# Rotation tables of the state-space batches in two buffers, outputs of a batch behind the next one's chunk inputs, four tiles for the gates

## The chip, the cores and the metric

One NeuronCore of a Trainium2 chip runs the whole kernel. The metric is device time in microseconds (us), the median of a few runs. TensorE is called PE here (its weight loads PEld), VectorE DVE, ScalarE ACT, GpSimd POOL, and the queue that issues most transfers SP. Each engine works through its own list of instructions in order, and engines wait for each other at semaphores.

## The reference, cut to what matters

One encoder layer over 16 meta tokens and 1024 tokens, in float32: a norm, one wide projection `w_in`, a state-space mixer (S5), differential attention, a gated sum of the two, and a feed-forward block. The change lies in the mixer and in the gate columns of the projection.

```
proj = hn @ w_in[layer]                      # columns: u 512, q, k 1024 each, v 1024, gates 2 x 1024
g_s5 = sigmoid(proj[..., OFF_GS:OFF_GA]);  g_attn = sigmoid(proj[..., OFF_GA:IN_COLS])
y = s5_mixer(u, ...)                         # 32 groups of 16 channels, 64 complex states, 2 directions
  bu_re, bu_im = einsum('blgc,gpc->lbgp', ug, b_re[dr]), einsum(..., b_im[dr])
  xr, xi = coef * bu                         # complex
  s = associative_scan(a * s_prev + x)       # along the 1040 tokens; reversed for direction 1
  y_dir = einsum(sr, c_re) - einsum(si, c_im)
y = gelu(y + d_skip * u)
```

## The kernel before, in words

The mixer is blocked: 1040 tokens are 130 chunks (`NJ`) of 8, and the 32 groups are worked through in **8 batches** of 4 groups. A batch is a generator, `s5_batch`, cut by `yield` into nine steps, called s0 to s8 here:

- **s0**: PE multiplies `Gm` (input matrix) and `c1` into `pk`; ACT copies it to `kt`. **s1**: PE transposes `Gm` (`pg`), ACT copies to `GT`; POOL builds the next batch's `Gm` (6 instructions, lines 541 to 543).
- **s2**: POOL builds `Hm` (6 instructions); SP moves `kt` into `M` (8 transfers); PE computes the chunk inputs `px`, ACT copies them to `Xr`, `Xi` (8 copies); SP loads the next batch's `U` (8 transfers).
- **s3**: DVE rotates `Xr`, `Xi` by the tables `TC`, `TS` (cosine and sine of each chunk's phase): six instructions of 128x520, called *the rotation*; then 8 scans. **s4**: DVE rotates back and writes `Sx`, 16 instructions of some 256 elements (*the Sx work*).
- **s5**: POOL builds the next batch's `TC` and `TS` by doubling (`s5_table`): 2 memsets and 48 instructions, most of them tiny. **s6**: PE transposes `M`, ACT copies it to `MT`.
- **s7**: PE sums `py` from `MT`, `Hm` and `Sx`; ACT squares, DVE multiplies. **s8**: ACT's Tanh, DVE writes `yt`, SP stores it to `yd` (4 transfers).

`TC` and `TS` have one buffer each, as have `Gm`, `Hm`, `M`, `Xr`, `Xi`; `U` and `yt` have two. Batch 0's table is built on DVE, the others on POOL.

The order is written out by hand. The steps of all batches make one list, `side`; from batch 1 on, s0 and s1 of a batch stand ahead of s7 and s8 of the batch before. `weave` hands one side step out after about each half-step of the main list, which is PE's own work: gate units 0 to 5 (`gate_steps`, 8 half-steps of 12 matmuls each), two value units (`v_steps`, *the V steps* here), gate unit 6. So every step has a place on every engine's list. A gate group ends in ACT's Tanh into `gt` (two buffers, pool `vg`); units 0 to 3 add DVE's +1.

Each unit's weights are split ahead of time into `wh` (ACT cast) and `wl` (a 128x1024 subtraction, line 174, on DVE): `unit` places the two halves of the next unit's split inside the present one. The unit ahead of the first gate unit is `U_U[1]`, woven with `s5_params` (the `gen_p` steps), a long run of small DVE instructions that ends in `dd`. The pool `utp` holds `ut`, the staging tile of the state-space inputs on their way to `ud` in memory.

Of the kernel before, what the change touches and what calls it, by code (L numbers as in the profile page):

```python
# [9 lines left out]
F32 = mybir.dt.float32  # L10
# [17 lines left out]
NJ = L // 8  # L28
# [23 lines left out]
def tile_hybrid_encoder(ctx, tc, A, out, dbg=None, stop=None):  # L52
    nc = tc.nc
# [74 lines left out]
    def weave(main, *sides, part=1.0):  # L128

        total = part * sum(w for w, _ in main)  # L130
        done = [0] * len(sides)
        t = 0.0
        for w, fn in main:
            fn()
            t += w
            for i, s in enumerate(sides):
                while done[i] < len(s) and done[i] + 1 <= len(s) * t / total + 1e-9:
                    s[done[i]]()
                    done[i] += 1
        for i, s in enumerate(sides):  # L140
            for fn in s[done[i]:]:
                fn()

    def steps_of(gen, n):

        return [lambda: next(gen, None) for _ in range(n)]
# [17 lines left out]
    def w_hi_part(i, h):  # L164
        if i < len(wviews):
            if h == 0:
                wtile[i] = (wp.tile([128, 2, 1024], F32R, tag="wh", name=f"wh{i}"),
                            wp.tile([128, 2, 1024], F32R, tag="wl", name=f"wl{i}"))
            nc.scalar.copy(wtile[i][0][:, h], wtile[i, h])

    def w_lo_part(i, h, eng):
        if i < len(wviews):
            hi, lo = wtile[i]
            eng.tensor_tensor(out=lo[:, h], in0=wtile.pop((i, h)), in1=_f(hi[:, h]), op=ALU.subtract)  # L174

    def w_split(i, h, eng=None):
        w_hi_part(i, h)
        w_lo_part(i, h, eng or nc.vector)

    def w_next(i, h):  # L180
        w_split(i + 1, h)
        w_dma(i + 2, h)

    def unit(i, steps):

        n = len(steps)
        at_ = {max(1, n // 6): 0, max(2, n // 2): 1}
        outl = []
        for j, (w, fn) in enumerate(steps):
            outl.append((w, fn))  # L190
            if j + 1 in at_:
                outl.append((0.0, lambda h=at_[j + 1]: w_next(i, h)))
        return outl

    def w8(i, k, c0, n):
# [3 lines left out]
    def cols(w, c0):  # L199
        v = w[:, c0:c0 + 256].rearrange("(h k p) n -> h p k n", h=2, p=128)  # L200
        return add_w(v[0], v[1])
# [3 lines left out]
    U_U = [cols(w_in, OFF_U + 256 * u) for u in range(2)]  # L205
# [19 lines left out]
    vg = pa.enter_context(tc.tile_pool(name="vg", bufs=2))  # L225
# [58 lines left out]
    def v_steps(u):  # L284
# [14 lines left out]
            later(vd[:, c0:c0 + P, 256 * u:256 * u + 256].rearrange("z p n -> p z n"), _f(vv[:P]), 1 if u < 2 else 2)  # L299
        return [(2.6 if t < NT else 1.7, lambda t=t, **k: step(t, **k)) for t in range(NT + 1)]  # L300

    def gate_steps(u, apart=False):
        ps_ = {}

        def half(c, t):
            ps_[c, t] = chan_group(U_G[u], c, NM + 512 * t, 512, None, (0, KD // 2))

        def mm(c, t):
            chan_group(U_G[u], c, NM + 512 * t, 512, ps_[c, t], (KD // 2, KD))

        def step(c, t):
            mm(c, t)
            fin(c, t)

        def fin(c, t):
            n0 = 256 * u + 128 * c
            ps = ps_[c, t]
            gt = vg.tile([128, 512], F32, tag="gt", name="gt")
            nc.scalar.activation(gt, ps, AF.Tanh, scale=0.5)
            if n0 < D:  # L320
                V.tensor_scalar(out=gt, in0=gt, scalar1=1.0, scalar2=None, op0=ALU.add)
                nc.sync.dma_start(gd[n0 // D, n0 % D:n0 % D + 128, 512 * t:512 * t + 512], gt)
            else:
                (nc.sync if apart else nc.scalar).dma_start(gd[n0 // D, n0 % D:n0 % D + 128, 512 * t:512 * t + 512], gt)
        if apart:
            return [[lambda c=c, t=t, f=f: f(c, t) for c in range(2) for t in range(2) for f in fs] for fs in ((half, mm), (fin,))]
        return [(2.6, lambda c=c, t=t, f=f: f(c, t)) for c in range(2) for t in range(2) for f in (half, step)]

    def u_steps(u):
        ut = {}  # L330

        def step(c, t0, n):
            if t0 == 0:
                ut[c] = utp.tile([128, 8, NJ], F32, tag="ut", name="ut", bufs=1)
            ps = chan_group(U_U[u], c, t0, n)
            nc.scalar.copy(ut[c][:, :, t0 // 8:(t0 + n) // 8], ps.rearrange("p (j t) -> p t j", t=8))
            if t0 + n == L:
                nc.scalar.dma_start(ud[256 * u + 128 * c:256 * u + 128 * c + 128], ut[c])
        return [(3.6, lambda c=c, t0=t0, n=n: step(c, t0, n)) for c in range(2)
                for t0, n in ((0, 344), (344, 352), (696, 344))]  # L340
# [187 lines left out]
    def s5_tile(tag, shape, b, bufs=1):  # L528
        return s5.tile(shape, F32, tag=tag, name=f"{tag}{b}", bufs=bufs)

    def s5_mats(P, b, which):

        g0 = GB * b
        G = nc.gpsimd
        tm = s5_tile("tm", [128, GB, 8, 16], b)
        o = P[which, b] = s5_tile(which, [128, 2, GB, 128], b)
        xr, xi, m1, m2 = [P[z] for z in (("gr", "gi", "b1", "b2") if which == "Gm" else ("hr", "hi", "c1", "c2"))]
        for d in range(2):
            c = slice(32 * d + g0, 32 * d + g0 + GB)
            o4 = o[:, d].rearrange("p g (t c) -> p g t c", t=8)  # L540
            G.tensor_tensor(out=o4, in0=_ins(xr[:, c, :], 3, 16), in1=_ins(m1[:, c, :], 2, 8), op=ALU.mult)
            G.tensor_tensor(out=tm, in0=_ins(xi[:, c, :], 3, 16), in1=_ins(m2[:, c, :], 2, 8), op=ALU.mult)
            G.tensor_tensor(out=o4, in0=o4, in1=tm, op=ALU.add)
# [6 lines left out]

    def s5_table(P, b):

        TC, TS = s5_tile("TC", [128, 2, 2, NJ], b), s5_tile("TS", [128, 2, 2, NJ], b)
        tt = s5_tile("tt", [128, 2, 2, 64], b)
        P["T", b] = TC, TS
        G = nc.gpsimd if b else V
        G.memset(TC[:, :, :, 0:1], 1.0)
        G.memset(TS[:, :, :, 0:1], 0.0)
        e2 = P["e2"].rearrange("p n z (r g) -> p n z r g", r=2)
        for lv in range(8):  # L560
            n = 1 << lv
            m = min(n, NJ - n)
            er = _ins(e2[:, lv, 0, :, 2 * b:2 * b + 2], 3, m)
            ei = _ins(e2[:, lv, 1, :, 2 * b:2 * b + 2], 3, m)
            xr, xi = TC[:, :, :, 0:m], TS[:, :, :, 0:m]
            yr, yi = TC[:, :, :, n:n + m], TS[:, :, :, n:n + m]
            t_ = tt[:, :, :, 0:m]
            for o, u, v, op in ((yr, er, ei, ALU.subtract), (yi, ei, er, ALU.add)):
                G.tensor_tensor(out=o, in0=xr, in1=u, op=ALU.mult)
                G.tensor_tensor(out=t_, in0=xi, in1=v, op=ALU.mult)  # L570
                G.tensor_tensor(out=o, in0=o, in1=t_, op=op)

    def s5_batch(P, b):
# [24 lines left out]
        if b + 1 < 8:  # L598
            s5_mats(P, b + 1, "Gm")
        yield  # L600
        s5_mats(P, b, "Hm")
        Hm = P["Hm", b]
        M = tl("M", [128, GB, 128])
        for t in range(8):
            nc.sync.dma_start(M[16 * t:16 * t + 16], kt[:, :, 16 * (7 - t):16 * (7 - t) + 128])
# [2 lines left out]
        for gp in range(2):  # L608
            for d in range(2):
                ps = pst([128, 2, NJ], "sm", "px")  # L610
                for pr_ in range(2):
                    nc.tensor.matmul(ps[:, pr_], GT[:, d, 2 * pr_ + gp], U[:, 2 * pr_ + gp], start=True, stop=True)
                o = slice(64 * gp, 64 * gp + 64)
                nc.scalar.copy(Xr[o, d], ps[0:64])
                nc.scalar.copy(Xi[o, d], ps[64:128])
        if b + 1 < 8:
            s5_load(P, b + 1)
        yield
        TC, TS = P["T", b]
        fl = lambda z: z.rearrange("p a b j -> p (a b j)")  # L620
        Rr, Ri, t5 = tl("Rr", [128, 2, 2, NJ + 1]), tl("Ri", [128, 2, 2, NJ + 1]), tl("t5", [128, 2, 2, NJ])
# [20 lines left out]
        for o, x1, t1_, x2, t2_, op in ((0, Rr, TC, Ri, TS, ALU.subtract), (64, Ri, TC, Rr, TS, ALU.add)):  # L642
            for d in range(2):
                s = 1 + 2 * d
                n = 128 - d
# [79 lines left out]
    put, put2 = ExitStack(), ExitStack()  # L725
# [105 lines left out]
    gen_p = s5_params(P5)  # L831
# [39 lines left out]
    w_split(2, 1)  # L871
    w_dma(3, 1)
    v1[NT][1]()
    weave(unit(U_U[0], u_steps(0)) + unit(U_U[1], u_steps(1)), steps_of(gen_p, 24))
    pprm.close()
    put.close()
    s5 = ps5.enter_context(tc.tile_pool(name="s5", bufs=1))
    s5_load(P5, 0)
    s5_mats(P5, 0, "Gm")
    s5_table(P5, 0)  # L880
    side = []
    for b in range(8):
        steps = steps_of(s5_batch(P5, b), 9)
        n = len(side) - 2 if b else 0
        side[n:n] = steps[:2]
        side += steps[2:]
    side[0:0] = [lambda: None]
    main = []
    for u in range(7):
# [4 lines left out]
            main.insert(len(main) - 6, (0.0, later))  # L894
    weave(main, side, part=0.98)
    ps5.close()
    put2.close()
    pvv.close()


# [162 lines left out]
    side = []  # L1063
    for u in range(4):
        if u == 3:
            load_head(0)
        for is_k in (True, False):
            w2 = w2s.pop(0) + (w2s.pop(0) if is_k else [])
            weave(unit((U_K if is_k else U_Q)[u], qk_steps(u, is_k)), side, w2, part=0.85 if u == 3 and not is_k else 1.0)
            side = steps_of(qk_post(u, is_k, u == 3 and not is_k), 6)  # L1070
# [480 lines left out]
    for j in range(3, NP + 1):  # L1551
# [13 lines left out]
        h = at_(1, LC)  # L1565
        if h is not None:
            load_head(h + 1)
        h = at_(3, LC)
        if h is not None:
            load_q(h + 1, 1)  # L1570
        h = at_(3, LP - 4)
        if h is not None:
            load_v(h + 1)
        h = at_(3, LS + 7)
        if h is not None and h < H - 3:
            o_st(h)
        h = at_(3, LS + 2)
# [4 lines left out]
        h = at_(3, LS)  # L1582
# [157 lines left out]
    side = []  # L1740
    for t in range(2):
# [4 lines left out]
        side = n_steps(t)  # L1746
# [354 lines left out]
```

## Time and profile before

| what | value |
|---|---|
| median of 3 runs | 1966.68 us (1963.84 to 1968.21) |
| the profiled execution's own time, and its span | 1969.38 us, 1967.6 us |
| PE busy | 94% of the span |
| DVE, ACT, POOL busy | 65%, 44%, 44% |
| mean granted TensorE clock | 0.977 of full speed |

Times inside the profile count from the start of the span. PE is the bound of most of the span; the batches run from about 137 to 465 us, and there the slices of the profile show PE at 7 or 8 tenths in turn with full slices. A busy share of PE counts a slow matmul (at half clock) as fully as a fast one.

### The profile page before, as it was taken

The numbers are of one execution on the slowest core, as the hardware profiler recorded it, in microseconds if no ns is written. First come the engines' busy times: TensorE is split into PE (matmuls) and PEld (weight loads), VectorE is DVE, ScalarE is ACT, GpSimd is POOL, SyncE is SP. The second block draws the span as 40 slices with busy tenths as digits, with TensorE's granted clock in tenths as the row PEclk, the third lists the DMA queues.
The fourth block names the chain that finished last, engine by engine and source line by source line (L and its number), as shares of the span: only waits on it lengthen the run. The fifth ranks groups of instructions, "written<-read, shape, count | busy, mean of one in ns | idle before, by whom it ended". The sixth has DMA issues, their size and how long they took to land. (4 is left out here: it accounts for less than half of the span.)

```text
span 1967.6 us, 31150 instructions
## 1 busy us (share of the span) xinstructions
PE 1846.1 (94%) x11306; PEld 1653.7 (84%) x11306; DVE 1278.4 (65%) x2623; ACT 865.6 (44%) x1581; POOL 868.3 (44%) x921
## 2 busy tenths in 40 slices
PE   7989887888999989999999998999899999999999
PEld 7977776788999879999999877998688887788887
DVE  6697777665543578999999865358544545654453
ACT  4323232232333357777677732235455554433332
POOL 3147887881423237677777700003665654410000
PEclk9999998998999999999999999999999999999999
DMA  7423222234677845455555334532544447985653
GB/s 213 123 71 98 70 75 76 87 93 143 230 242 245 287 136 164 122 148 161 156 154 153 116 97 140 208 125 74 187 147 148 159 148 259 364 299 185 201 203 118
DMA packets 230537, 315.90 MB, mean 161 GB/s; under 512 B 39560, under 2 KB 140472, under 8 KB 230344
## 3 DMA queue, kind: packets, MB, share of 16 engines
q1 hardware_dynamic: 209952, 283.14, 45.7%
q10 hardware_dynamic: 20432, 30.78, 4.4%
q8 instruction: 89, 1.46, 0.3%
q14 instruction: 64, 0.52, 0.1%
HBM read 212.28 MB, written 99.48 MB: 158 GB/s over the span
## 5 line engine op out<-in xcount | busy, mean ns | idle before, releaser
L92 PE MATMUL ps<-wh,hnh 128*128 128x256 f32 x768 | 221.3, 288 | 4.5 <-DVE qraw L949 4.2
L89 DVE TENSOR_TENSOR fp<-fr,fp 128x1024 fp32r<-128x1024 f32 x112 | 141.9, 1314 | 127.4 <-ACT fp L88 126.8
L93 PE MATMUL ps<-wh,hnl 128*128 128x256 f32 x768 | 218.5, 285 | 5.5 <-DVE hnl L89 5.5
L94 PE MATMUL ps<-wl,hnh 128*128 128x256 f32 x768 | 218.2, 284 | 0.4 <-POOL wl L174 0.4
L88 ACT CAST fp<-fr 128x1024 fp32r<-128x1024 f32 x112 | 110.4, 1051 | 181.0 <-PE pf L94 164.8
L94 PE MATMUL pf<-fp 128*128 128x512 f32 x448 | 174.6, 390 | 1.3 <-DVE fp L89 1.3
L92 PE MATMUL pf<-fp 128*128 128x512 f32 x448 | 174.5, 390 | 0.6 <-ACT fp L88 0.6
L93 PE MATMUL pf<-fp 128*128 128x512 f32 x448 | 174.3, 389 | 0.0
L1161 ACT ACTIVATE E<-E,st 128x1040 f32<-128x1040 f32 x128 | 149.4, 1167 | 46.5 <-DVE st L1155 37.0
L1155 DVE CUSTOM_DVE_ANT_0 E<-S,Tb,st 128x344 f32<-128x344 f32 x256 | 146.8, 574 | 27.8 <-PE S L1144 6.3
L1177 POOL TENSOR_TENSOR w<-E,E 128x1040 f32<-128x1040 f32 x64 | 155.4, 2429 | 5.3
L92 PEld LDWEIGHTS ps<-wh,hnh 128*128 128x128 f32 x768 | 147.1, 192 | 7.4 <-DVE qraw L949 4.9
L93 PEld LDWEIGHTS ps<-wh,hnl 128*128 128x128 f32 x768 | 147.3, 192 | 6.0 <-DVE hnl L89 5.9
L94 PEld LDWEIGHTS ps<-wl,hnh 128*128 128x128 f32 x768 | 147.3, 192 | 0.6 <-POOL wl L174 0.6
L93 PE MATMUL ps<-hnh,wl 128*128 128x512 f32 (+2 forms) x352 | 133.3, 379 | 6.8 <-DVE wl L174 6.8
L1143 PE MATMUL S<-K,Q 128*128 128x344 f32 (+1 forms) x384 | 135.2, 353 | 1.3 <-DVE st L1155 0.8
L92 PE MATMUL ps<-hnh,wh 128*128 128x512 f32 (+2 forms) x352 | 135.9, 386 | 0.0
L94 PE MATMUL ps<-hnl,wh 128*128 128x512 f32 (+2 forms) x352 | 132.3, 376 | 0.0
L89 DVE TENSOR_TENSOR swl<-w1r,swh 128x512 fp32r<-128x512 f32 x70 | 77.1, 1134 | 73.8 <-ACT swh L88 73.8
L1194 ACT CAST W<-wt 128x384 fp32r<-128x384 f32 x192 | 89.3, 481 | 80.4 <-PE wt L1184 72.5
L1144 PE MATMUL S<-K,Q 128*128 128x344 f32 (+1 forms) x384 | 123.7, 323 | 0.0
L1175 POOL TENSOR_SCALAR E<-E,st 128x1040 f32<-128x1040 f32 x64 | 73.5, 1149 | 97.3 <-DVE st L1168 56.8
(425 smaller groups left out, 5364.8 us busy)
## 6 DMA issues: line engine op xcount, KB each, us to landing
fr<-ad SPq DMA_DIRECT2D x56, 512.0 KB
ad<-r SPq DMA_DIRECT2D x91, 256.0 KB
raw<-in_w_in_dram SPq DMA_DIRECT2D x44, 512.0 KB
w<-in_w_ff_dram SPq DMA_DIRECT2D x32, 512.0 KB
wd<-w SPq DMA_DIRECT2D x32, 512.0 KB
Q<-qd SPq DMA_DIRECT2D x128, 128.0 KB
fr<-wd SPq DMA_DIRECT2D x32, 512.0 KB
w1r<-in_w_ff_dram SPq DMA_DIRECT2D x28, 512.0 KB
```

What stands on the lines that cost most here:

```text
L88: nc.scalar.copy(hi, src)
L89: (eng or nc.vector).tensor_tensor(out=lo, in0=src, in1=_f(hi), op=ALU.subtract)
L92: nc.tensor.matmul(o, l[0], r[0], start=start, stop=False, **kw)
L93: nc.tensor.matmul(o, l[1], r[0], start=False, stop=False, **kw)
L94: nc.tensor.matmul(o, l[0], r[1], start=False, stop=stop, **kw)
L1143: nc.tensor.matmul(ps[:, 0:n], qa[:, qs], k, start=True, stop=False)
L1144: nc.tensor.matmul(ps[:, 0:n], qb[:, qs], k, start=False, stop=True)
L1155: V.tensor_tensor_reduce(out=t["E", m][:, c0:c0 + n], in0=t.pop(("S", m, c))[:, 0:n], in1=HT[h]["Tb"][:, b0:b0 + n], scale=1.0, scalar=mn ...
L1161: nc.scalar.activation(t["E", m], t["E", m], AF.Exp, bias=t["mn"][:, m:m + 1], scale=-1.0, accum_out=t["Z"][:, m:m + 1])
L1175: nc.gpsimd.tensor_scalar(out=E1, in0=E1, scalar1=t["cf"][:, 0:1], scalar2=0.0, op0=ALU.mult, op1=ALU.add)
L1177: nc.gpsimd.tensor_tensor(out=w[:, 112:], in0=_rev(E0), in1=_rev(E1), op=ALU.add)
L1194: nc.scalar.copy(WT[p, g][:, :, 0, x], IT[i]["tp", g])
```

## The change

Five edits. `TC` and `TS` get two buffers each. In `s5_batch` one `yield` moves: the old s2 ended after the `U` load, now it ends after the `Xr`, `Xi` copies, and the `Hm` matrices and the `U` load begin s3. The list `side` puts three steps (s0, s1, s2) of a batch ahead of s7 and s8 of the one before, where it put two. `unit` takes an engine, and the unit `U_U[1]` gives its two `wl` subtractions (those of gate unit 0) to POOL. Gate tiles alternate between `vg` and the batches' pool `s5`, two buffers in each; to make room, `utp` is closed ahead of the batches.

```
-    def unit(i, steps):
+    def unit(i, steps, eng=None):
...
-                outl.append((0.0, lambda h=at_[j + 1]: w_next(i, h)))
+                outl.append((0.0, lambda h=at_[j + 1]: w_next(i, h, eng)))
...
-            gt = vg.tile([128, 512], F32, tag="gt", name="gt")
+            ng[0] += 1
+            gt = (s5 if s5 and ng[0] % 2 else vg).tile([128, 512], F32, tag="gt", name="gt", bufs=2)
...
-        TC, TS = s5_tile("TC", [128, 2, 2, NJ], b), s5_tile("TS", [128, 2, 2, NJ], b)
+        TC, TS = s5_tile("TC", [128, 2, 2, NJ], b, 2), s5_tile("TS", [128, 2, 2, NJ], b, 2)
...
         yield
-        s5_mats(P, b, "Hm")
-        Hm = P["Hm", b]
         M = tl("M", [128, GB, 128])
...
                 nc.scalar.copy(Xi[o, d], ps[64:128])
+        yield
+        s5_mats(P, b, "Hm")
+        Hm = P["Hm", b]
         if b + 1 < 8:
             s5_load(P, b + 1)
-        yield
...
-    weave(unit(U_U[0], u_steps(0)) + unit(U_U[1], u_steps(1)), steps_of(gen_p, 24))
+    weave(unit(U_U[0], u_steps(0)) + unit(U_U[1], u_steps(1), nc.gpsimd), steps_of(gen_p, 24))
     pprm.close()
     put.close()
+    put2.close()
...
-        side[n:n] = steps[:2]
-        side += steps[2:]
+        side[n:n] = steps[:3]
+        side += steps[3:]
```

**POOL, ahead of the batches.** Before, after the last instructions of `s5_params` (`bt`) POOL's list goes straight to batch 0's `Gm`:

```order
L462 TENSOR_TENSOR bt_1192<-l_517,ci 128x1024
L463 TENSOR_TENSOR bt_1191<-bt_1191,bt_1192 128x1024
L541 TENSOR_TENSOR Gm_1644<-pgr,bt_1190 128x512
L542 TENSOR_TENSOR tm_1643<-pgi,bt_1191 128x512
L543 TENSOR_TENSOR Gm_1644<-Gm_1644,tm_1643 128x512
```

With the change:

```order
L465 TENSOR_TENSOR bt_1192<-l_517,ci 128x1024
L466 TENSOR_TENSOR bt_1191<-bt_1191,bt_1192 128x1024
L174 TENSOR_TENSOR wl_1459<-raw_0_1073,wh_1458 128x1024
L174 TENSOR_TENSOR wl_1459<-raw_1_1201,wh_1458 128x1024
L544 TENSOR_TENSOR Gm_1645<-pgr,bt_1190 128x512
L545 TENSOR_TENSOR tm_1644<-pgi,bt_1191 128x512
L546 TENSOR_TENSOR Gm_1645<-Gm_1645,tm_1644 128x512
```

The two weight subtractions of gate unit 0 stand between them now, and are gone from DVE's list; the rest of POOL's list keeps its order.

**ACT, from batch 1's `GT` on.** Before, the Square and Tanh of batch 0's output (`y`) stand ahead of batch 1's copies of the chunk inputs (`Xr`, `Xi`, four pairs):

```order
L596 COPY GT_2075<-pg 128x512 x2
L671 ACTIVATE y_2124<-py 128x512
L319 ACTIVATE gt<-ps 128x512
L675 ACTIVATE y_2124<-y_2124 128x512
L169 CAST wh_2053<-raw_1_1861 128x1024
L614 COPY Xr_2184<-px 64x260
L615 COPY Xi_2185<-px 64x260
```

With the change they stand behind them:

```order
L599 COPY GT_2076<-pg 128x512 x2
L615 COPY Xr_2120<-px 64x260
L616 COPY Xi_2121<-px 64x260
...
L322 ACTIVATE gt<-ps 128x512
L674 ACTIVATE y_2172<-py 128x512
L169 CAST wh_2054<-raw_1_1845 128x1024
L678 ACTIVATE y_2172<-y_2172 128x512
```

The chunk inputs move up by two places of the list, the outputs back by one; on PE `px` and `py` change in the same way. The rotation's place on DVE stays.

**SP, the same place.** Before (`raw` are weights, `gd` the gates):

```order
L680 DMA yd<-yt_2123 8x16x128 x4
L161 DMA raw_1_2152<-in_w_in_dram 128x4x256
L605 DMA M_2175<-kt_2032 16x4x128 x8
L548 DMA U_2206<-ud 16x4x130 x8
L322 DMA gd<-gt 128x512 x2
```

With the change:

```order
L606 DMA M_2111<-kt_2033 16x4x128 x8
L325 DMA gd<-gt 128x512
L161 DMA raw_1_2178<-in_w_in_dram 128x4x256
L683 DMA yd<-yt_2171 8x16x128 x4
L325 DMA gd<-gt 128x512
L551 DMA U_2223<-ud 16x4x130 x8
```

The transfers of `M` no longer stand behind the output of the batch before; those of `U` still do.

## Rows read from the trace of the kernel before

**Rows 1.** Windows of 20 us: length, busy (x count) by engine, clock, DMA share, GB/s

```profile
290.00:310.00 20.00, 14.86 (x70) 12.77 (x69) 15.71 (x30) 3.32 (x6) 13.01 (x35) 0.83 0.21 66
310.00:330.00 20.00, 20.00 (x113) 16.39 (x111) 12.12 (x10) 8.38 (x17) 19.22 (x29) 1.00 0.30 81
```

**Rows 2.** Waits, 130 to 480 us: waiter <- releaser: total us, times, longest

```profile
POOL TC L557 <- DVE t L85: 47.5, 7, 8.2
...
PE py L666 <- DVE Sx L651: 19.5, 5, 4.4
...
DVE t L85 <- POOL TC L571: 14.9, 4, 7.7
...
PE ps L93 <- DVE wl L174: 6.5, 1, 6.5
```

**Rows 3.** Tile TC: count: ns min/median/max, first and last start

```profile
L557 POOL MEMSET TC<- x7: 104/105/108, 177.2 to 423.7; 128x4 f32 x7
```

**Rows 4.** Timeline of POOL, 290 to 335 us: start, length, instruction [idle before]

```profile
293.12 1.29 POOL L543 TENSOR_TENSOR Hm<-Hm,tm 128x512 f32<-128x512 f32 x1
300.39 0.10 POOL L557 MEMSET TC<- 128x4 f32 x1 [5.98 <-DVE t L85]
...
301.13 0.48 POOL L570 TENSOR_TENSOR tt<-TS,e 128x4 f32<-128x4 f32 x1
301.69 1.29 POOL L571 TENSOR_TENSOR TC<-TC,tt 128x4 f32<-128x4 f32 x1
...
304.07 0.20 POOL L570 TENSOR_TENSOR tt<-TS,e 128x4 f32<-128x4 f32 x1
...
318.44 1.06 POOL L541 TENSOR_TENSOR Gm<-pgr,bt 128x512 f32<-128x512 f32 x1
319.46 1.52 POOL L542 TENSOR_TENSOR tm<-pgi,bt 128x512 f32<-128x512 f32 x1
...
333.33 1.29 POOL L543 TENSOR_TENSOR Hm<-Hm,tm 128x512 f32<-128x512 f32 x1
```

**Rows 5.** Timeline of DVE, the same stretch

```profile
300.70 0.85 DVE L651 TENSOR_TENSOR Sx<-t,q 64x254 f32<-64x254 f32 x2
301.60 0.06 DVE L652 MEMSET Sx<- 128x4 f32 x1
301.69 2.36 DVE L174 TENSOR_TENSOR wl<-raw,wh 128x1024 fp32r<-128x1024 f32 x2
...
309.02 0.69 DVE L677 SCALAR_TENSOR_TENSOR yt<-y,py 128x512 f32<-128x512 f32 x1 [0.70 <-ACT y L675]
...
317.44 0.70 DVE L85 TENSOR_TENSOR t<-Xr,TC 128x520 f32<-128x520 f32 x1 [7.70 <-POOL TC L571]
318.52 1.54 DVE L85 TENSOR_TENSOR q<-Xi,TS 128x520 f32<-128x520 f32 x1 [0.38 <-POOL TS L571]
...
331.19 4.05 DVE L638 TENSOR_TENSOR_SCAN Ri<-rho,Xi 128x130 f32<-128x130 f32 x4
```

**Rows 6.** Timeline of DVE, up to and in batch 0

```profile
111.45 2.27 DVE L85 TENSOR_TENSOR ei<-er,ei 128x32 f32<-128x32 f32 x1
...
133.64 2.35 DVE L174 TENSOR_TENSOR wl<-raw,wh 128x1024 fp32r<-128x1024 f32 x2
...
170.11 1.36 DVE L638 TENSOR_TENSOR_SCAN Ri<-rho,Xi 128x130 f32<-128x130 f32 x4
```

**Rows 7.** Timeline of POOL, ahead of batch 0

```profile
111.24 2.43 POOL L463 TENSOR_TENSOR bt<-bt,bt 128x1024 f32<-128x1024 f32 x1
136.89 1.05 POOL L541 TENSOR_TENSOR Gm<-pgr,bt 128x512 f32<-128x512 f32 x1 [23.21 <-DVE TS L558]
```

**Rows 8.** Timeline of PE, batch 0's `pk`

```profile
143.80 0.22 PE L587 MATMUL pk<-Gm,ct 128*16 128x16 f32 x2 [1.10 <-POOL Gm L543]
```

**Rows 9.** Timeline of DVE, V steps, ahead of the rotations of batches 6 and 7

```profile
401.62 1.80 DVE L174 TENSOR_TENSOR wl<-raw,wh 128x1024 fp32r<-128x1024 f32 x1 [3.85 <-ACT wh L169]
...
442.32 2.33 DVE L174 TENSOR_TENSOR wl<-raw,wh 128x1024 fp32r<-128x1024 f32 x1 [4.33 <-ACT wh L169]
```

More of the change, by code (lines that the diff above doesn't have):

```diff
@@ L178, in w_split, with w_next @@
         w_lo_part(i, h, eng or nc.vector)
-    def w_next(i, h):
-        w_split(i + 1, h)
+    def w_next(i, h, eng=None):
+        w_split(i + 1, h, eng)
         w_dma(i + 2, h)
-    def unit(i, steps):
+    def unit(i, steps, eng=None):
         n = len(steps)
@@ L300, in v_steps @@
         return [(2.6 if t < NT else 1.7, lambda t=t, **k: step(t, **k)) for t in range(NT + 1)]
+    ng, s5 = [0], None
     def gate_steps(u, apart=False):
@@ L896, in tile_hybrid_encoder @@
     ps5.close()
-    put2.close()
+    s5 = None
     pvv.close()
```

## The prediction, made before the changed kernel ran

> **What bounds the kernel now.** I read three views, in this order. The windows come first. Over the batches, stretches of 20 us alternate between a PE that is full at clock 1.00 and one that is busy for 14.86 us at a mean clock of 0.83 [rows 1]. PE therefore loses about 5.1 us of each 40 to idleness, and some more to half clock after it. The waits say on what: PE waits at `py` for DVE's `Sx` (19.5 us in 5 waits), and POOL waits 47.5 us in 7 waits at the first instruction of the table, for DVE's last reads of the old one [rows 2]. The table starts 7 times from 177.2 to 423.7 us [rows 3], so a batch takes (423.7 - 177.2) / 6 = 41.1 us.
>
> The timelines show the loop that makes 41.1. POOL ends `Hm` at 294.4, idles 5.98 us until the `Sx` work lets go of the table, then builds the next table from 300.39 to 318.44 [rows 4]. DVE is done with `yt` at 309.7 and waits 7.70 us for that table; it starts the rotation at 317.44, ends the scans at 335.24 [rows 5], and does the `Sx` work until about 342, where the next table begins. Two pieces stand end to end: table 18 us, rotation to the end of `Sx` 23 to 24 us. PE's wait at `py` is a result of this loop. With two buffers the table need not wait for `Sx`.
>
> **The change, part by part.**
>
> *The second table buffer.* It takes POOL's wait away: 47.5 us in 7, the first 8.2, the others (47.5 - 8.2) / 6 = 6.55 each [rows 2]. What is late next? POOL's own list. Without its waits a batch holds 41.1 - 6.55 = 34.6 us of POOL work. DVE needs 23 to 24 us from rotation to the end of `Sx`, and 8 more from there (301.66) to the end of `yt` (309.71) [rows 5]: 32 to 33. PE is busy for 34.9 of 40 us, part of it at half clock [rows 1], so it needs less than that. POOL is the longest of the three.
>
> *What that does to POOL.* POOL is idle during most of the `Sx` work now. After the change the table follows `Hm` at once and runs under it. The rows show what that costs: while DVE works on `Sx`, a table instruction of 4 elements takes 0.48 us and one under a `wl` takes 1.29, each ending just behind DVE's instruction; alone it takes 0.20 [rows 4, 5]. DVE keeps its own pace of 0.425 us an instruction there. So one table instruction passes per `Sx` instruction, and loses 0.425 - 0.20 = 0.23 to 0.48 - 0.20 = 0.28 us. I take 0.25. Three of the 16 `Sx` instructions already meet the table today, so 13 x 0.25 = 3.3 us come back per batch. Bounds: nothing, if the tiny instructions slip between; and 13 x 0.43 = 5.6, if POOL loses all of DVE's time. The rows lie nearer the middle.
>
> The result for a batch is 34.6 + 3.3 = 37.9 us instead of 41.1, and POOL is the bound.
>
> The Trainium skill speaks against the change here. Its page "SBUF — State Buffer", section "Who interferes with whom", says that a DVE instruction with two SBUF inputs and a GpSimd instruction that reads SBUF exclude each other, the later one blocking until the first has finished. The trace agrees in the direction (the 0.48 and 1.29 us above). By that page a full overlap buys nothing, since the work only queues; that is the last rival below.
>
> *Start of the batches.* Gate unit 0's two `wl` leave DVE, where they end at 136.0 us (133.64 + 2.35) [rows 6], and PE's 6.5 us wait for them goes [rows 2]. They go to POOL, ahead of batch 0's `Gm`, while DVE still runs its small instructions. POOL's work stops those: one of 32 elements took 2.27 us beside a POOL instruction of 128x1024 that took 2.43 [rows 6, 7]. Two such are added, so DVE's run, which ended at 133.64, ends at 133.64 + 2 x 2.2 = 138.0 instead of 136.0 with the `wl`. `Gm` waits for DVE's `dd` at the end of that run and started 0.9 us after the `wl` [rows 6, 7]; it would now start near 138.9, 2.0 us later. PE's `pk` waits for it even now [rows 8], so PE's wait only moves there. I count **+2.0**. Bounds: -2.35 if POOL does not slow DVE, +2.5 if it blocks it fully. The staging tile's last transfer, for which the batches' pool now waits too, should be hidden under the same wait; if not, it adds what it is late.
>
> *First batch.* -8.2, +3.3, and six scans that POOL did not meet before at 0.25 each: **-3.4**.
>
> *Batches up to the fifth rotation.* Four times -6.55 + 3.3: **-13.0**.
>
> *V steps.* There the rotations start several us after their tables are done, so the table does not bind. They stand behind a `wl` that waits for ACT's cast, 3.85 and 4.33 us, and that itself takes 1.80 and 2.33 [rows 9]. ACT's cast stands behind the copies of `Xr`, `Xi`, which the change moves two places up. I count 1.5 and 2.5 us: **-4**. Bounds: 0 and -8.2, the whole of both waits.
>
> *Moves that I cost at nothing.* `px` and its copies ahead of `py`, and the `M` transfers ahead of `yd`: they move the same instructions within a loop whose longest member is POOL, and the transfers have several us of cover before `M` is transposed. `Hm` and the `U` load, one step later: on POOL they keep their order, and `U` has a whole batch to arrive. The output one step later: DVE's 37.9 - 33 = 5 us of slack covers 2.8 us of one more half-step; if that slack is gone, it costs up to that per batch. The gate tiles: PE waits for no gate tile in the list [rows 2]. Their cost and gain are 0.
>
> *Sum:* +2.0 - 3.4 - 13.0 - 4 = -18.4 us, say -18. Against the profiled execution's own 1969.38 us this is 1951; the median of the runs is 2.7 lower, so 1966.7 - 18 = **1949 us**.
>
> **The rivals.**
>
> *More is gained.* The tiny table instructions cost nothing under `Sx`, and a batch falls to POOL's 34.6 us. Then the gain is 8.2 + 4 x 6.55 = 34.4, less 2.0, plus 4: 36 us, 1930 us. For it: DVE would then sit at 33, PE below 35, so nothing else stops it first. Against it: every row where POOL meets DVE shows POOL longer. PE at full clock gives the floor of this case: if every idle 5.1 us of 8 batches went, 41 us, 1926.
>
> *Nothing is gained.* The critical wait moves to another place of the same length: the `Sx` work becomes longer, or the output's later place on the lists keeps DVE from starting the rotation when the table is ready. Then 1963 to 1970. For it: in the 41.1 us, DVE waits for the table only 14.9 us in 4 waits [rows 2], 3.7 on average; what DVE can gain from an early table is no more than this unless its other waits shrink with it. Against it: those others are waits for PE and ACT, which the loop holds back too.
>
> *Slower: the `Sx` work falls beside POOL's long instructions.* Beside `Gm` and `Hm`, DVE gets one instruction through per POOL instruction. The scans show it: four take 4.05 us there (1.01 each) and 1.36 alone (0.34) [rows 5, 6], and a 128x520 product takes 1.54 instead of 0.70 [rows 5]. If the 16 `Sx` instructions fell there, they would take 16 x (1.01 - 0.34) = 10.7 us longer, DVE's loop would be 33 + 10.7 = 43.7, that is 2.6 over 41.1, and five batches with the start give +15: 1982 us. Today 14 DVE instructions (rotation and scans) use up POOL's 12 long ones just before the `Sx` work begins. The case decides itself when `Hm`, which waits for the later `py`, slips by more than about 10 us behind the rotation's start. I see 5 us of room at least before that.
>
> *Slower by queueing.* If all two-input work of DVE and all of POOL's excluded each other in full, a batch would hold POOL's lone time, about 15.5 for the table (18.05 less what it loses to `wl` and `Sx`) and 2 x 6.9 for `Gm` and `Hm` (136.89 to 143.80 [rows 7, 8]), plus DVE's 6 x 0.70 + 8 x 0.34 + 16 x 0.425 + some 4 for `wl` and output, 17.7: 47.0 us, 5.9 above today; five batches make 1966.7 + 2 + 30 = 1999 us. That is the skill's rule taken whole. Against it: today's 34.6 us of POOL already hold about 11 us of such DVE work, and `Hm` under the scans is barely longer (1.29 at 293.12 and at 333.33 [rows 4]).
>
> **How the numbers follow.** Forecast (POOL bound at 36.5 to 39 us a batch, 1941 to 1958): 0.50. More gained: 0.20. Nothing: 0.16. Slower, either way: 0.10. The remaining 0.04 is a gain between forecast and nothing. Less than 0.2%, 3.9 us, could hardly be told from no change here; so faster 0.74, same 0.16, slower 0.10. The range runs from the larger gain, 1926, to no change, 1967. It leaves out the slower cases and half of the case of nothing. The forecast's own range is 1941 to 1958.
>
> **What would show it.** Right: POOL's wait at the table's first instruction is gone, tables start about 38 us apart, POOL is busy nearly throughout from batch 1 on, the table lasts 21 to 22 us instead of 18, and the rotation still starts when the table ends. `Gm` of batch 0 starts near 139, with PE waiting at `pk` instead of at gate unit 0's `wl`. Wrong: tables that start 41 us apart although the wait is gone (it moved); `Sx` instructions of 1 us (the slow rival); PE full from window to window (the larger gain). The weakest terms are the 3.3 us per batch and the V steps.

## The result, and the profile after

The changed kernel takes 1942.34 us (median of 4 runs, 1940.91 to 1943.93), the kernel before beside it 1967.45 us: a ratio of 0.9875 with a 95% interval of 0.9858 to 0.9892, 25.1 us less. The forecast was 1949, 18 us less. The profiled execution took 1943.93 us, its span is 1942.1 us.

The engines' line of the page, busy us (share of the span) and instructions:

```profile
PE 1839.4 (95%) x11306; PEld 1647.8 (85%) x11306; DVE 1275.4 (66%) x2621; ACT 865.7 (45%) x1581; POOL 893.5 (46%) x923
```

PE does the same work, DVE all but the two subtractions that POOL takes. POOL's busy time grows by 25 us, of which two weight subtractions are 4.8 and the seven longer tables some 20. The two windows of [rows 1], after:

```profile
290.00:310.00 20.00, 20.00 (x106) 16.97 (x106) 11.88 (x21) 6.49 (x14) 18.98 (x39) 1.00 0.45 131
310.00:330.00 20.00, 17.92 (x107) 14.39 (x106) 19.73 (x27) 8.75 (x19) 19.25 (x31) 1.00 0.17 55
```

PE's gap in these 40 us is 2.1 us instead of 5.1, and the clock is 1.00 in both. They are among the fuller stretches: from 247.7 to 285.6 us PE is busy for 33.3 of 37.9 us, at a mean clock of 0.91. In the 40 us POOL is busy for 38.2, 32.2 before. The waits from 130 to 480 us, as in [rows 2], and the starts of the table, as in [rows 3]:

```profile
DVE t L85 <- POOL TC L574: 9.7, 3, 3.8
...
PE pk L589 <- POOL Gm L546: 8.6, 1, 8.6
...
PE py L670 <- DVE Sx L655: 5.2, 3, 1.8
```

```profile
L560 POOL MEMSET TC<- x7: 95/101/126, 172.1 to 396.2; 128x4 f32 x7
```

POOL's wait of 47.5 us at the table's first instruction is gone from the list, and so is PE's 6.5 us for the weights of gate unit 0. Tables start (396.2 - 172.1) / 6 = 37.35 us apart; 41.1 before. POOL's timeline shows a batch without any gap, from the end of `Hm` through the table to the next `Gm`:

```profile
208.65 1.30 POOL L546 TENSOR_TENSOR Hm<-Hm,tm 128x512 f32<-128x512 f32 x1
209.88 0.10 POOL L560 MEMSET TC<- 128x4 f32 x1
...
216.11 0.51 POOL L572 TENSOR_TENSOR TC<-TC,e 128x32 f32<-128x32 f32 x1
...
217.41 0.48 POOL L572 TENSOR_TENSOR TS<-TC,e 128x32 f32<-128x32 f32 x1
...
218.87 1.28 POOL L572 TENSOR_TENSOR TC<-TC,e 128x64 f32<-128x64 f32 x1
...
230.51 0.20 POOL L572 TENSOR_TENSOR TS<-TC,e 128x8 f32<-128x8 f32 x1
...
231.60 1.06 POOL L544 TENSOR_TENSOR Gm<-pgr,bt 128x512 f32<-128x512 f32 x1
```

DVE in the same stretch: the `Sx` work, a `wl`, the output, and the next rotation, which still starts when the table is ready:

```profile
217.38 0.85 DVE L654 TENSOR_TENSOR Sx<-t,q 64x254 f32<-64x254 f32 x2
...
218.71 1.28 DVE L174 TENSOR_TENSOR wl<-raw,wh 128x1024 fp32r<-128x1024 f32 x1
...
230.59 0.70 DVE L85 TENSOR_TENSOR t<-Xr,TC 128x520 f32<-128x520 f32 x1 [3.77 <-POOL TC L574]
```

The table runs under the `Sx` work now and is longer for it: the 0.48 and 0.51 us beside `Sx` at 32 elements per partition (0.24 alone, before), the 1.28 beside `wl` at 64 (0.29 alone); the 0.20 is an instruction of 8 alone. `Sx` keeps its 0.42 us an instruction. The start of the batches, POOL and PE, as in [rows 7, 8]:

```profile
114.73 2.38 POOL L174 TENSOR_TENSOR wl<-raw,wh 128x1024 fp32r<-128x1024 f32 x1
119.96 2.44 POOL L174 TENSOR_TENSOR wl<-raw,wh 128x1024 fp32r<-128x1024 f32 x1 [2.85 <-ACT wh L169]
139.93 1.05 POOL L544 TENSOR_TENSOR Gm<-pgr,bt 128x512 f32<-128x512 f32 x1 [17.52 <-DVE dd L525]
```

```profile
143.39 0.61 PE L589 MATMUL pk<-Gm,ct 128*16 128x128 f32 x2 [8.58 <-POOL Gm L546]
```

`Gm` starts 3.0 us later than before; 1.1 of that was there after the first 66 us already (the same PE instruction starts that much later in this execution), so 1.9 belong to the change.

And DVE in the V steps, ahead of the seventh rotation (rotations are counted like batches, from 0), as in [rows 9]:

```profile
420.48 0.69 DVE L680 SCALAR_TENSOR_TENSOR yt<-y,py 128x512 f32<-128x512 f32 x1 [0.70 <-ACT y L678]
421.42 1.97 DVE L174 TENSOR_TENSOR wl<-raw,wh 128x1024 fp32r<-128x1024 f32 x1 [0.25 <-ACT wh L169]
423.33 1.54 DVE L85 TENSOR_TENSOR t<-Xr,TC 128x520 f32<-128x520 f32 x1
424.79 1.79 DVE L85 TENSOR_TENSOR q<-Xi,TS 128x520 f32<-128x520 f32 x1
```

The wait of 4.33 us for ACT's cast is 0.25. But something else stands there: batch 6's output `yt` ends at 421.2, right ahead. The last `py` ends at 443.3 us, 465.2 before.

### The profile page after: what moved, and what is told of

Its sections match the earlier page's. It is cut to its first block, busy times and chain, and to the rows that moved or that the text cites. A ratio compares the mean times of both kernels' runs of the same rounds, so it can differ in the third digit from the quotient of the medians.

```text
span 1942.1 us, 31135 instructions
## 1 busy us (share of the span) xinstructions
PE 1839.4 (95%) x11306; PEld 1647.8 (85%) x11306; DVE 1275.4 (66%) x2621; ACT 865.7 (45%) x1581; POOL 893.5 (46%) x923
```

## The experiments

Each was timed beside the kernel before, the two on the same chip. Before took 1964.2 to 1964.5 us in these sessions, so 0.9875 stands for about 1940 us; compare ratios.

**One edit alone, and all but this one.** `e1_tables_only` is the kernel before with this edit; `e2_one_table` is the changed kernel without it:

```
-        TC, TS = s5_tile("TC", [128, 2, 2, NJ], b), s5_tile("TS", [128, 2, 2, NJ], b)
+        TC, TS = s5_tile("TC", [128, 2, 2, NJ], b, 2), s5_tile("TS", [128, 2, 2, NJ], b, 2)
```

> The kernel before with the second buffer for TC and TS alone; the other four edits are left out. Theory (the second table lets POOL go on under the Sx work, and POOL's own list becomes the bound): tables start 37 to 38 us apart, the wait of POOL at the first instruction of the table is gone, the time is that of the changed kernel less its later start (-2) and without the gain in the V steps (+4 to +5): 1945 us (1942 to 1949). Rival A (the gain comes from the chunk inputs ahead of the outputs): most of it is missing, 1959 to 1967. Rival B (the gain comes from the four gate tiles or from the weight split on POOL): also 1959 or more.

> The changed kernel with one buffer for TC and TS; all other edits stay. Theory: POOL's wait at the table's first instruction comes back (some 40 us in 7), tables are 41 us apart again, only the V steps' gain (-4 to -5) and the later start (+2) are left against the kernel before: 1962 to 1966 us, PE's wait at py back near 20 us. Rival A (the moved steps carry the gain): 1941 to 1950.

Measured: `e1_tables_only` 1937.84 us, 0.9868 (0.9854 to 0.9881), lower than expected; `e2_one_table` 1965.58 us, 1.001 (1.000 to 1.002). The table starts and, of `e2_one_table`, POOL's wait:

```profile
L557 POOL MEMSET TC<- x7: 98/105/108, 169.0 to 391.7; 128x4 f32 x7
```

```profile
L560 POOL MEMSET TC<- x7: 106/106/108, 179.9 to 426.1; 128x4 f32 x7
```

```profile
POOL TC L560 <- DVE t L85: 47.8, 7, 8.8
```

37.1 us between tables in the one, 41.0 in the other, with the whole wait back. The second table buffer makes the gain, and the other four edits together make none. That is against the V-step term of the prediction, which hung on one of them.

**The other edits, one by one.** `e3_wl_on_dve` gives the two subtractions back to DVE (`unit(U_U[1], u_steps(1))` without `nc.gpsimd`). `e5_steps_back` undoes the moved steps. `e6_two_gates` takes both gate tiles from `vg`:

```
-            gt = (s5 if s5 and ng[0] % 2 else vg).tile([128, 512], F32, tag="gt", name="gt", bufs=2)
+            gt = vg.tile([128, 512], F32, tag="gt", name="gt")
```

> The changed kernel with the two weight subtractions of gate unit 0 on DVE again. Theory (they cost about 2 us as they stand, since they stop DVE's small instructions ahead of the first Gm): 1940.4 us, 1.9 faster than the changed kernel; the first Gm starts near 138 us instead of 139.9, PE waits for the subtraction on DVE again (6.5 us) and less at pk. Rival (taking PE's wait of 6.5 us away is a gain): 2 to 6 us slower than the changed kernel. Second rival (hidden either way): within 0.5 us.

> The changed kernel with the moved steps undone: Hm and the U load end s2 again, and two steps of a batch, not three, stand ahead of the outputs of the one before. Theory after the first four runs (the move gains nothing: what it takes from the wait for ACT's cast ahead of the seventh rotation it gives back, since the output of batch 6 now stands on DVE's list ahead of that rotation, and py of batch 6, which releases Hm, ends 4 us later): 1938 to 1941 us, as the tables alone (1937.8) plus the later start of up to 2.9 us. The prediction's term (the move gains 4 us in the V steps): 4 us slower than the changed kernel, 1945 to 1947.

> The changed kernel with the gate tiles from the pool vg alone, two of them. Prediction's term (0): 1941 to 1944 us. Rival (four tiles take waits of ACT for the gates' transfers away): 2 us slower or more, 1945 and up. Second rival (four tiles let ACT run ahead with gates and hold the mixer's copies back): 2 us faster, 1940 or less.

Measured: `e3_wl_on_dve` 1941.84 us, 0.9885 (0.9869 to 0.9901); `e5_steps_back` 1941.47 us, 0.9883 (0.9865 to 0.9902); `e6_two_gates` 1940.46 us, 0.9876 (0.9859 to 0.9894). None can be told from the changed kernel. For the gate tiles this is the forecast. `e3_wl_on_dve` is a miss of mine: `Gm` does start at 137.45, and tables 2.7 to 3.0 us earlier than after, but the seventh rotation starts at 423.00 against 423.33: in both it stands behind batch 6's output, and the lead is gone. `e5_steps_back` decides little by its interval, but its trace has the last `py` end at 443.6 us, 443.3 after (an execution that was 1.0 us later than it ahead of the batches); the trace of `e1_tables_only`, which has the old steps too, shows why the move wins so little. DVE at the same place as the last fence above:

```profile
417.51 0.67 DVE L677 SCALAR_TENSOR_TENSOR yt<-y,py 128x512 f32<-128x512 f32 x1
422.88 1.23 DVE L174 TENSOR_TENSOR wl<-raw,wh 128x1024 fp32r<-128x1024 f32 x1 [4.70 <-ACT wh L169]
424.04 0.69 DVE L85 TENSOR_TENSOR t<-Xr,TC 128x520 f32<-128x520 f32 x1
424.65 0.69 DVE L85 TENSOR_TENSOR q<-Xi,TS 128x520 f32<-128x520 f32 x1
```

The wait for ACT is there, 4.70 us, and the rotation starts only 0.7 us later than after. Its products take 0.69 instead of 1.54 and 1.79, because `Hm` of batch 7 ran from 413.7 to 420.9, ahead of it. `Hm` has one buffer and waits until `py` of batch 6 has read the old one: `py` ended at 413.6 here, and at 417.6 after, where `px` stands ahead of it; there `Hm` ran until 426.0, beside the rotation. What the move takes from one wait it gives back at two places.

**Is POOL's list the bound?** `e4_pool_more` is the changed kernel with one more POOL instruction for each direction of `Hm`:

```
             G.tensor_tensor(out=o4, in0=o4, in1=tm, op=ALU.add)
+            if which == "Hm":
+                G.tensor_tensor(out=tm, in0=_ins(xi[:, c, :], 3, 16), in1=_ins(m2[:, c, :], 2, 8), op=ALU.mult)
```

> The changed kernel with two more POOL multiplications of 128x512 in each batch, at the end of Hm, into tm, which nobody reads after; this adds work that the result does not need, some 1.2 to 1.5 us each. Theory (POOL's list bounds the batches from the first to the fifth or sixth): tables start 2.4 to 3.0 us further apart, 39.8 to 40.4, and the time grows by 10 to 17 us to 1952 to 1959. Rival (PE, which is full in many windows now, or DVE is the bound): less than 4 us, POOL only loses slack.

Measured: 1955.51 us, 0.9959 (0.9944 to 0.9974), some 16 us more by the ratios, as the theory had it. Its table starts:

```profile
L562 POOL MEMSET TC<- x7: 98/100/382, 174.1 to 409.3; 128x4 f32 x7
```

(409.3 - 174.1) / 6 = 39.2 us, 1.9 more a batch where 2.4 to 3.0 were expected (the two took 1.06 us each in most batches); the rest of the loss comes in the V steps (the last `py` ends at 458.6, 15.3 later than after). POOL has no gap from table to table, so work added to its list lengthens the batches at once.

**The V steps.** `e8_long_in_6` puts four long multiplications at the end of `Hm` of batch 6 alone, into `e1_tables_only`:

```
+            if which == "Hm" and b == 6:
+                for _ in range(2):
+                    G.tensor_tensor(out=tm, in0=_ins(xi[:, c, :], 3, 16), in1=_ins(m2[:, c, :], 2, 8), op=ALU.mult)
```

> The kernel before with two table buffers (as e1_tables_only), and four more POOL multiplications of 128x512 at the end of Hm of batch 6 alone, into tm, which nobody reads after: unused work of some 5 us, at a place where POOL's table for the seventh rotation has about 10 us of slack. Theory (the V steps gained because POOL, run ahead, no longer puts Gm and Hm beside the rotation and the scans of batches 6 and 7): the sixth rotation with its scans takes 12 to 14 us again instead of 9.0, and the time is 3 to 5 us above the tables alone, 1941 to 1943. Rival (the V steps gained only by what came earlier ahead of them): POOL's slack takes it, less than 1 us.

Measured: 1940.07 us, 0.9873 (0.9855 to 0.9891), 2.2 us above `e1_tables_only` by the medians and 1.0 by the ratios, with intervals that overlap: by the time alone inconclusive. The trace shows the mechanism. At the end of batch 6's rotation, POOL's last long instruction and DVE's scans, first of `e1_tables_only`, then of `e8_long_in_6`:

```profile
390.11 1.64 POOL L543 TENSOR_TENSOR Hm<-Hm,tm 128x512 f32<-128x512 f32 x1
```

```profile
394.21 1.38 DVE L638 TENSOR_TENSOR_SCAN Rr<-rho,t 128x130 f32<-128x130 f32 x4
395.50 1.36 DVE L638 TENSOR_TENSOR_SCAN Ri<-rho,Xi 128x130 f32<-128x130 f32 x4
```

```profile
394.38 2.87 POOL L546 TENSOR_TENSOR tm<-phi,ct 128x512 f32<-128x512 f32 x2
```

```profile
396.26 2.23 DVE L641 TENSOR_TENSOR_SCAN Rr<-rho,t 128x130 f32<-128x130 f32 x4
398.42 1.36 DVE L641 TENSOR_TENSOR_SCAN Ri<-rho,Xi 128x130 f32<-128x130 f32 x4
```

Rotation and scans take 9.0 us in the one (387.91 to 396.9) and 12.3 in the other (387.52 to 399.8); before they took 14.3, 403.7 to 418.0. The last `py` ends 2.8 us later, though this rotation began 0.4 earlier: 3.2 us are lost in between, about what rotation and scans lose. The two profiled executions end within 0.3 us of each other all the same (spans of 1935.8 and 1936.1 us), so what this is worth at the end of the kernel is not shown.

**A shorter table.** The loop of before is table plus rotation to `Sx`; a shorter table should be worth as much as a second buffer, and both together more. `e7_short_table` is `e1_tables_only` with cosine and sine in one tile, three instructions of a level instead of six half as large (`e2` gets -sine and sine, laid out by batch); `utp` is closed ahead of the batches, as in the change:

```
-            for o, u, v, op in ((yr, er, ei, ALU.subtract), (yi, ei, er, ALU.add)):
-                G.tensor_tensor(out=o, in0=xr, in1=u, op=ALU.mult)
-                G.tensor_tensor(out=t_, in0=xi, in1=v, op=ALU.mult)
-                G.tensor_tensor(out=o, in0=o, in1=t_, op=op)
+            G.tensor_tensor(out=y, in0=x, in1=er, op=ALU.mult)
+            G.tensor_tensor(out=t_, in0=_rev(x, 1), in1=ei, op=ALU.mult)
+            G.tensor_tensor(out=y, in0=y, in1=t_, op=ALU.add)
```

`e10_short_one` is this table with one buffer, `e12_short_pool_more` the addition of `e4_pool_more` on `e7_short_table`, `e11_short_moved` the moved steps on it, `e9_short_all_edits` all five edits on it.

> The kernel before with two table buffers (as e1_tables_only), and each table built as one tile of cosine and sine by three POOL instructions of a level in place of six half as large: 24 instructions and 2 memsets instead of 48 and 2; the same values, and one small DVE instruction more in each of eight parameter steps. Theory (POOL's list bounds the batches): the table falls from some 20 us to 14 to 16, tables start 32 to 35 us apart instead of 37.1 where POOL still binds, else DVE's loop of 32 to 33 us or PE does; 2 to 4 us less in each of five batches, 1918 to 1929 us, 10 to 20 faster than the tables alone. Rival (DVE or PE bounds already): the table gets shorter, but the time stays within 3 us of 1937.8.

> The kernel before, with its single table buffer and none of the five edits, and the short table of e7_short_table. Theory (the loop of before is the table plus the stretch from the rotation to the end of the Sx work, so that a shorter table is worth its difference in each of five batches): the table falls from 18 to about 13 us, tables start 36 to 37 us apart instead of 41.1, POOL's wait at the table's first instruction stays: 1938 to 1946 us, as much as the second buffer gives. Rival (another wait of before takes the gain): 1955 or more.

> The kernel e7_short_table with two more POOL multiplications of 128x512 in each Hm, which write tm a second time with the same values: 2.4 us and more of work per batch that the result does not need. Theory (with the short table POOL has about 1.0 to 1.4 us of slack in a batch of 33 us, its waits ahead of Gm, and PE bounds): 1 to 2 us more in four or five batches, 1929 to 1934. Rival (POOL still bounds): as much as in e4_pool_more, 13 us, 1938. Second rival (PE bounds with more slack on POOL than its waits show): under 2 us.

> The kernel e7_short_table with the moved steps of the change (outputs of a batch behind the next one's chunk inputs) and none of the other edits. Theory (PE is full, the move only changes who waits off the bound): within 3 us of 1925.4. Rival (DVE's wait of up to 4.4 us for the copies of Xr ahead of the rotation was what is left to win): 1915 to 1921.

> The changed kernel with the short table of e7_short_table, so all five edits together with it; the gate tiles are three (two in vg, one in the batches' pool), since the wider scratch tile leaves no room for four. Theory (with the short table PE is full in most windows of the batches, so that the other four edits have nothing to win): as e7_short_table, 1925.4, plus up to 3 us for the later start: 1924 to 1930. Rival (their gain was hidden behind POOL's list and comes out now): 1915 to 1921.

| kernel | median us | ratio | 95% interval |
|---|---|---|---|
| `e7_short_table` | 1925.43 | 0.9803 | 0.9786 to 0.9821 |
| `e10_short_one` | 1940.00 | 0.9874 | 0.9861 to 0.9888 |
| `e12_short_pool_more` | 1941.50 | 0.9879 | 0.9863 to 0.9894 |
| `e11_short_moved` | 1930.24 | 0.9835 | 0.9820 to 0.9849 |
| `e9_short_all_edits` | 1931.50 | 0.9833 | 0.9819 to 0.9846 |

`e7_short_table` is the fastest kernel of this study, 39 us below before. Its windows, as above:

```profile
290.00:310.00 20.00, 20.00 (x107) 16.43 (x106) 14.68 (x26) 8.32 (x16) 18.82 (x28) 1.00 0.44 131
310.00:330.00 20.00, 20.00 (x143) 18.14 (x141) 11.71 (x18) 8.41 (x19) 17.14 (x21) 1.00 0.21 69
```

PE is full in both. From the first table (167.4) to the sixth (329.6) a batch takes 32.4 us, and the table of batch 4, say, 15.1 (264.1 to 279.1). `e10_short_one` meets its forecast: one buffer and a short table give as much as the whole change, though its tables start 37.7 us apart ((404.2 - 177.9) / 6) and not 36 to 37: the table is 4.7 us shorter (13.2 on average), but the stretch from its end to the next one's start grew from 23.2 to 24.5. POOL's wait is longer there, and DVE does the `Sx` work beside an idle POOL:

```profile
POOL TC L558 <- DVE q L85: 56.3, 7, 9.9
```

`e12_short_pool_more` is a miss: 16 us more (15 by the ratios), not 4 to 8. The batch goes from 32.4 to 35.2 us ((347.3 - 171.3) / 5), by all that was added. What I took for slack of POOL were waits for PE, such as this one of `e7_short_table`, and they did not absorb the work:

```profile
280.52 1.15 POOL L542 TENSOR_TENSOR Gm<-pgr,bt 128x512 f32<-128x512 f32 x1 [1.39 <-PE pg L592]
```

POOL's list alone is not the bound there, however: in `e12_short_pool_more` POOL still waits 2.6 and 2.3 us for `pg` in two of these batches, and 3.81 and 3.29 us for `py` in two others, where PE in turn waits for DVE's `Sx`. PE's wait in `e7_short_table`, then both waits in `e12_short_pool_more`:

```profile
PE py L664 <- DVE Sx L649: 6.3, 3, 3.4
```

```profile
POOL Hm L542 <- PE py L666: 21.5, 3, 14.4
...
PE py L666 <- DVE Sx L651: 14.9, 4, 4.6
```

In batches 1 and 3 the `Sx` work takes 14.6 us from the last scan's end, where it took 11.9 and 13.0; in batch 1 nearly half of it lies beside `Gm`. So at least part of the loss runs from POOL through DVE to PE, and comes back to POOL as a wait. With the short table the three engines wait for each other in turn; that the longer list alone would have cost as much is not shown.

`e11_short_moved` and `e9_short_all_edits` are slower than `e7_short_table` by 5 and 6 us (6 each by the ratios; the intervals of the first two just touch), both above what I expected: here the moved steps cost. POOL's wait at `Hm`, first in `e7_short_table`, then in `e11_short_moved`:

```profile
POOL Hm L542 <- PE py L664: 17.3, 2, 17.0
```

```profile
POOL Hm L542 <- PE py L664: 31.1, 6, 15.8
```

Without the longest wait of each it is 15.3 us instead of 0.3. As in the V steps, but now in most batches, `px` ahead of `py` lets go of `Hm`'s buffer later.

## Why the prediction was right, and where it was not

**The bound.** Right: POOL's wait goes, its own list follows as the bound. Predicted 34.6 + 3.3 = 37.9 us a batch, measured 37.35; `e4_pool_more` confirms that POOL binds. The table lengthened from 17.9 to 20.8 us on average (means of the seven), 2.9 instead of 3.3. Four batches are worth 13.4 us (rotation 5 moves from 359.4 to 343.2, less what the first table had), 13.0 predicted.

**Start.** +1.9 at `Gm`, predicted +2.0, and PE's wait did move to `pk`. But the trace of `e3_wl_on_dve` shows that these 2 us do not reach the end of the changed kernel (its times alone cannot tell 2 us); what a late start costs was counted as if nothing downstream had slack.

**First batch.** Mis-sized: predicted -3.4, measured -5.8 (the table's end moves from 196.1 to 193.3, less 1.9 and 1.1 of later start). The first table lengthened by 2.3 us, from 18.9 to 21.2, where 3.3 + 1.5 were counted. Scans beside tiny POOL instructions cost POOL less than `Sx` does: under the scans of batch 1 the next table's first instructions took 0.20 to 0.37 us (210.06 to 211.5), some 0.1 more than alone, where 0.25 was counted. For six scans that is 0.9 of the 2.5 us counted too many; where the rest comes from is open.

**V steps.** Here the step failed: "ACT's cast stands behind the copies of `Xr`, `Xi`, which the change moves two places up. I count 1.5 and 2.5 us". The two waits for the cast did shrink, from 3.85 and 4.33 us to 0.25 each, but the output of the batch before stands there now, and with the steps undone the last `py` ends nearly as early (443.6 us in `e5_steps_back`, 443.3 after): with the 1.0 us of different starts the move is worth about 1 us in the traces, not 4, and none that the times show. That the size is near is luck (from rotation 5 to the last `py` the lead over the kernel before grows from 16.2 to 21.9, 5.7 us). With the second buffer alone that growth is 11.0 us (14.3 to 25.3). POOL, run ahead, has done with `Gm` and `Hm` before the rotation and the scans of batches 6 and 7, which take 9.0 and 6.6 us instead of 14.3 and 9.2; those of batch 5 take 13.5 instead of 17.3, and the three together are 11.8 us shorter. I had read the scans' 4.05 us beside POOL and 1.36 alone [rows 5, 6] as a danger for `Sx` only; they were a gain to be had. The moved steps give some of it back: in the changed kernel the three take 17.2, 12.7 and 8.5 us, only 2.4 less than before, and what brings the other 3.3 of its 5.7 us no run here shows. That the shorter rotations are the cause of the 11.0 us is tested in part: `e8_long_in_6` brings 3.3 of 5.3 us of one of them back, and the last `py` with it, in the trace.

**The rest.** The four terms measure +1.9 - 5.8 - 13.4 - 5.7 = -23.0 us where -18.4 were forecast; with the 1.1 us that this execution was late before the change acts, that is the lead of 21.9 at the last `py`. At the end of the profiles the lead is 25.5. The difference comes from 601 to 725 us, and it comes in `e2_one_table` too (from 1.2 us behind to 3.6 ahead), whose batches gain nothing: the profiled execution of before seems to have been slow there, and it stood 2.7 us above its median.

**The rivals.** *More is gained* did not come: tiny instructions do cost. *Nothing* did not, since DVE's other waits shrank with the table's: from the first to the sixth table DVE is idle for 11.5 us a batch before and 7.4 after, 4.1 less, of which the wait for the table itself is about 1 (14.9 us in all before, 9.7 after). *Slower by queueing*, the rule of the Trainium skill's page "SBUF — State Buffer", section "Who interferes with whom", taken whole, gave 47.0 us a batch and 1999 us, where 37.35 and 1942 were measured; the traces agree that the engines hold each other up, not that it adds up like that. The `Sx` instructions take 0.427 us on average after, 0.418 before, so it is POOL that pays, some 3 us a batch. *`Sx` beside long instructions* did not come in the changed kernel. In `e7_short_table` it did, though not because `Hm` slipped: beside `Sx` stand the short table's widest levels (0.68 to 1.26 us an instruction from 271.9 us on) and then `Gm`. `Sx` instructions take 0.66 us on average there, and the stretch from the last scan's end to the end of `Sx` is 13.0 us in batch 3 (271.6 to 284.6), 6.7 after. It cost little, since the rotation and the scans, now clear of `Gm` and `Hm`, take 7.2 us instead of 17.7: from the rotation's start to the end of `Sx` it is 20.1 us, 24.4 after.

## What to carry to other kernels

Before a second buffer is given to a table, read what the builder's own list holds without the wait: that sum, with a surcharge for what it will meet on the shared stretch, was the new period within 2%. Where two engines alternate in a loop, shortening the one that builds can be worth as much as the buffer (here three instructions for six: 24 us against 26), and both together gave 39 us, less than their sum. A step moved ahead of another delays what that other one releases: look which single-buffered tile waits for it, here `Hm` behind `py`.

## What the runs showed of the hardware

A table instruction on POOL of 4 to 32 elements per partition, which takes 0.20 to 0.25 us alone, takes 0.36 to 0.47 in the median (0.51 at most) beside DVE's back-to-back instructions of the `Sx` work, and those keep their 0.42 (0.427 on average). Beside POOL's instructions of about 1 us and more it is DVE that pays: in `e7_short_table` `Sx` takes 0.66 instead of 0.42 on average and 1.39 at most, and in the kernels before and after four scans take 4.05 to 5.16 us instead of 1.36. So in these runs the two engines cost each other little when the short instructions are on POOL (2.9 us a batch), and much when they are on DVE (13.0 us instead of 6.7 for the `Sx` work above).
